# One of four sums of weights per pair by an accumulating load, with turned signs and a fourth raw buffer

## The chip, the cores and the metric

The kernel runs on 1 core of a Trainium2 chip. Its time is the device time of one execution in microseconds (us). TensorE (PE) does the matrix products, VectorE (DVE) and ScalarE (ACT) the work on elements, GpSimd (POOL) small things and some loads, and SyncE (SP) issues most of the loads from HBM.

## The reference

Two layers, each an FFN, a token mixer and a second FFN, with a layer norm behind each; 256 tokens of 1024 numbers in float32.

```python
D_MODEL = 1024; SEQ = 256; DEPTH = 2; D_FF = 2816

def swiglu(x, wg, wu, wd):
    return (jax.nn.silu(x @ wg) * (x @ wu)) @ wd

for l in range(DEPTH):
    x = layer_norm(ALPHA * x + 0.5 * swiglu(x, ffn_wg[l, 0], ffn_wu[l, 0], ffn_wd[l, 0]), ln_g[l, 0], ln_b[l, 0])
    m = token_mix(x, w_in[l], w_out[l], ...)
    x = layer_norm(ALPHA * x + m, ln_g[l, 1], ln_b[l, 1])
    x = layer_norm(ALPHA * x + 0.5 * swiglu(x, ffn_wg[l, 1], ffn_wu[l, 1], ffn_wd[l, 1]), ln_g[l, 2], ln_b[l, 2])
```

The token mixer (sparse attention, pooling, gated linear attention) is not touched by the change.

## The kernel before

**Products in three matmuls.** Each float32 operand is split in two, `h` and `l`: ACT copies it to the reduced type (`wh`, L217 or L229), DVE subtracts that from the original (`wl`, L218 or L230). A product is then three matmuls: high by high, high by low, low by high. All weights pass this way, 393 halves of 128x1024 (512 KB) in all: SP loads the half into a buffer `raw` (three of them, L222), ACT and DVE split it, and PE uses it for both halves of the tokens. The buffer is free for the next load when `wl` is done. `wh` and `wl` have rings of 8 buffers each.

**An FFN.** The 2816 columns of the hidden layer are 11 chunks of 256 gate and 256 up columns. `glu` (units `a`, `b` in the plan) makes one chunk from two weight units of two halves. `T0`, `T2`, ... transpose the gated result `hh` (or `cc`) of two chunks on PE and split it to `hi` and `lo` (L267, L268, called from `h_T`), and `d0`, `d1`, ... multiply it by the chunk's rows of the down weights and add to `accs`. `PLAN` (L41) is the order of these units on PE. It ends with `d7 T8`; then `end` runs d10, d8, d9 for the first 128 tokens, d10, d8, d9 for the others, and the layer norm (L342) follows each.

**Seven products for eight.** Three pairs of chunks per FFN (`S4`, `S6`, `S8`, so 12 pairs in all) are made by block products, "1 5 6 7 3 4 2" in this order, each of 12 matmuls. The inputs are cut in blocks of tokens and of inner index (`make_sums`, L310, forms the sums of x), the weights in b11, b12, b21, b22 of two halves each. `seven` (L135) forms the sums of weights: "5" takes b12 - b11, "6" takes b22 - (b12 - b11), "7" takes b22 - b12, "4" takes b21 less the sum of "6"; "1", "3" and "2" take b11, b22 and b21 as they are. Each sum is two DVE subtractions of 128x1024 (`less`, L145 to L147), in place in the tiles `fa` (b11) or `fb` (b12); `fc` is b22. b21 is loaded into two of the three `raw` buffers and stays there until "2" has been split. `plan` (L418) runs the products and adds up what PE leaves in PSUM (L462, L465, L468), and `gated` (L475) applies silu (ACT, L478) and the multiplication (DVE, L479).

**What sets the order.** Inside an FFN's plan PE's instructions are pinned to program order, and weight units are requested three ahead of their use, elsewhere one ahead. The order on the other engines is made by a scheduler when the kernel is built; on each engine it is then fixed, and an instruction that waits holds up all that stand behind it.

Of the kernel before, what the change touches and what calls it, by code (L numbers as in the profile page):

```python
# [10 lines left out]
def _warn_once_fixed(msg, *args, **kwargs):  # L11
# [7 lines left out]
F32 = mybir.dt.float32  # L19
# [3 lines left out]
AF = mybir.ActivationFunctionType  # L23
ALU = mybir.AluOpType
# [14 lines left out]


PLAN = ("a2 T0 b2 S4 1 a3 5 b3 6 T2 d0 7 d1 3 4 2 S6 d2 1 5 T4 d3 6 a10 7 b10 3 4 2 "  # L41
        "S8 1 d4 5 T6 6 d5 T10 7 d6 3 4 2 d7 T8").split()

LAST = (10, 8, 9)
WARM = ((7, 512), (4, 128))
# [12 lines left out]
def build(ctx, tc, d):  # L58
    nc = tc.nc
    PE, ACT, DVE, POOL = nc.tensor, nc.scalar, nc.vector, nc.gpsimd  # L60

    cst = ctx.enter_context(tc.tile_pool(name="cst", bufs=1))
    wp = ctx.enter_context(tc.tile_pool(name="wp", bufs=1))
# [54 lines left out]
    for t in range(2):  # L118
        vbd.append(cst.tile([128, 2, 2, 64], F32, name=f"vbd{t}"))
        a = cst.tile([128, 4, 128], F32, name=f"at{t}")  # L120
# [11 lines left out]
    def gate_up(l, f, c, q):  # L132
        return [d["wgu"][l, f, c, 2 * q + h] for h in range(2)]

    def seven(l, f, c):  # L135


        b11, b12, b21, b22 = [], [], [], []

        def load(to, src, pool, name, tags, bufs):  # L140
            for a, tag in zip(src, tags):
                to.append(pool.tile([128, 1024], F32, name=name, tag=tag, bufs=bufs))
                last_dma[0] = nc.sync.dma_start(out=to[-1], in_=a)

        def less(a, b, to):  # L145
            for x, y, z in zip(a, b, to):
                DVE.tensor_sub(out=z, in0=x, in1=y)  # L147

        def parts(ts):
            return [split_tile(x, 1024) for x in ts]  # L150

        def f1():
            load(b11, gate_up(l, f, c, 0), mix, "fa", ("qs0", "qs1"), 1)
            return parts(b11)

        def f5():
            load(b12, gate_up(l, f, c + 1, 0), wp, "fb", ("fb0", "fb1"), 1)
            less(b12, b11, b11)
            return parts(b11)

        def f6():
            load(b22, gate_up(l, f, c + 1, 1), mix, "fc", ("pT", "pT"), 3)
            less(b22, b11, b11)
            return parts(b11)

        def f7():
            less(b22, b12, b12)
            return parts(b12)

        def f4():  # L170
            load(b21, gate_up(l, f, c, 1), wp, "raw", ("raw", "raw"), 3)
            less(b21, b11, b11)
            return parts(b11)

        return {"1": f1, "5": f5, "6": f6, "7": f7, "3": lambda: parts(b22), "4": f4, "2": lambda: parts(b21)}

    for l in range(L):
        def ffn_units(f):
# [33 lines left out]
    def split_tiles():  # L212
        return (wp.tile([128, 1024], F32R, name="wh", bufs=8), wp.tile([128, 1024], F32R, name="wl", bufs=8))
# [5 lines left out]
        return wh, wl  # L219

    def split_half(src, w, parts=1, between=None):
        raw = wp.tile([128, 1024], F32, name="raw", bufs=3)  # L222
        wh, wl = split_tiles()
        for i in range(parts):
            s = slice(i * w // parts, (i + 1) * w // parts)
            last_dma[0] = nc.sync.dma_start(out=raw[:, s], in_=src[:, s])
            if between:
                between[i]()
            ACT.activation(out=wh[:, s], in_=raw[:, s], func=AF.Copy)  # L229
            DVE.tensor_sub(out=wl[:, s], in0=raw[:, s], in1=wh[:, s].bitcast(F32))  # L230
        return wh, wl
# [63 lines left out]
    def make_xT(t, qs=(0, 1), sums=None):  # L295
        if 0 in qs:
            XT[t] = (act.tile([128, 8, 128], F32R, name=f"xh{t}"), act.tile([128, 8, 128], F32R, name=f"xl{t}"))
        xh, xl = XT[t]
        for q in qs:
            p = transposes(t, [X[t][:, (4 * q + i) * 128:(4 * q + i + 1) * 128] for i in range(4)], ("tr", "acc")[q])  # L300
            split(xh[:, 4 * q:4 * q + 4, :], xl[:, 4 * q:4 * q + 4, :], p.rearrange("p (a b) -> p a b", a=4))
            if sums is not None:
                if (t, q) != (1, 1):
                    f = sums[t, q] = mix.tile([128, 512], F32, name=f"a{t}{q}", tag=("c40", "c41", "at011")[2 * t + q], bufs=1)
                    ACT.activation(out=f, in_=p, func=AF.Copy)
                else:
                    f = sums["s"] = mix.tile([128, 512], F32, name="s1", tag="vblk", bufs=1)
                    DVE.tensor_add(out=f, in0=p, in1=sums[1, 0])

    def make_sums(sums):  # L310

        s1, a11, a12, a21 = sums["s"], sums[0, 0], sums[0, 1], sums[1, 0]
        big = cst.tile([128, 2, 2, 4, 128], F32R, name="sb", tag="s_w1")

        def parts(f, i):
            tl = cst.tile([128, 2, 4, 128], F32R, name=f"sa{i}", tag=("ksh", "ksl")[i]) if i < 2 else big[:, i - 2]
            split(tl[:, 0], tl[:, 1], f.rearrange("p (a b) -> p a b", a=4))
            return tl[:, 0], tl[:, 1]
        first = parts(s1, 0)
        DVE.tensor_sub(out=s1, in0=s1, in1=a11)  # L320
        DVE.tensor_sub(out=a21, in0=a11, in1=a21)
        DVE.tensor_sub(out=a12, in0=a12, in1=s1)
        yield first
        yield parts(s1, 1)
        yield parts(a21, 2)
        yield parts(a12, 3)
# [39 lines left out]
    class Ffn:  # L366
# [51 lines left out]
        def plan(self):  # L418
            a = [[tuple(p[:, 4 * q:4 * q + 4] for p in XT[t]) for q in range(2)] for t in range(2)]
            left = {"1": a[0][0], "2": a[0][1], "4": a[1][1]}  # L420
            sums = make_sums(self.sums)

            def f32():
                self.cc += 1
                return mix.tile([128, 512], F32, name="cc", tag=("vblk", "cc", "c40", "at011", "c41")[self.cc % 5], bufs=1)

            def copy(b):

                r = f32()
                ACT.activation(out=r, in_=b, func=AF.Copy)  # L430
                return r
            for x in PLAN:
                if x[0] == "S":
                    c = int(x[1:])

                    (w1, b1), (w5, b5) = self.bank(), self.bank()
                    if not m0 and c == 8:
                        with tc.issue_after(last_dma[0].ins):
                            late_constants()
                            m0.append(Mix(0))  # L440
                            ln_params(0, 0)
                elif x[0] in "abTd":
                    for t in range(2):
                        if x[0] == "T":
                            self.h_T(t, int(x[1:]) // 2)
                        elif x[0] == "d":
                            self.down(t, int(x[1:]))
                        else:
                            self.glu(t, int(x[1:]), "ab".index(x[0]))
                    continue  # L450
                else:
                    if x in "5673" and x not in left:
                        left[x] = next(sums)
                    self.product(b1 if x in "1674" else b5, left[x], x in "152")
                with tc.high_priority():
                    if x == "1":
                        c11 = copy(b1)
                    elif x == "6":
                        u = copy(b1)
                    elif x == "7":  # L460
                        c22 = copy(b1)
                        DVE.tensor_add(out=c22, in0=b5, in1=c22)  # L462
                        self.gated(1, c + 1, c22)
                    elif x == "3":
                        DVE.tensor_add(out=u, in0=b5, in1=u)  # L465
                        self.gated(0, c + 1, u)
                    elif x == "2":
                        DVE.tensor_add(out=c11, in0=b5, in1=c11)  # L468
                        self.gated(0, c, c11)
                        self.free.append(w5)  # L470
                    elif x == "4":
                        self.gated(1, c, b1, f32())
                        self.free.append(w1)

        def gated(self, t, c, x, to=None):  # L475
            if to is None:
                to = x
            ACT.activation(out=to[:, 0:256], in_=x[:, 0:256], func=AF.Silu)  # L478
            DVE.scalar_tensor_tensor(out=to[:, 0:256], in0=to[:, 0:256], scalar=0.5, in1=x[:, 256:512], op0=ALU.mult,  # L479
                                     op1=ALU.mult)  # L480
            self.hh.setdefault((t, c // 2), [None, None])[c % 2] = to

        def h_T(self, t, g):
# [521 lines left out]
    sums = {}  # L1005
    for l in range(L):
# [3 lines left out]
        out = [wout(m, t) for t in range(2)]  # L1010
        for op in ORDER.split():
            t = int(op[1]) if len(op) > 1 else 0
# [16 lines left out]
        sums = nxt  # L1029
# [85 lines left out]
```

## Time and profile before

| | |
|---|---|
| time, median of 3 runs | 982.41 us (982.23 to 983.89) |
| the profiled execution | 982.67 us, of which the trace's span is 980.9 |
| PE, DVE, ACT, POOL busy | 959.1, 843.2, 583.1, 34.8 us |
| moved by DMA | 178.80 MB, mean 182 GB/s |
| granted clock of PE, mean | 0.997 |

The profile is that of one execution. Times in it count from the start of the span. The first FFN ends at about 186 us, its mixer at 320, the second FFN at 487, the third at 669, the second mixer at 803.

### The profile page before, as it was taken

How to read it: one execution, taken by the hardware profiler on the slowest of the kernel's cores; microseconds unless marked ns; L12 is line 12 of the kernel's file. 1: busy time of each engine (PE TensorE's matmuls, PEld its weight loads, DVE VectorE, ACT ScalarE, POOL GpSimd, SP SyncE). 2: the span in 40 equal slices, each digit the busy share in tenths (PEclk: the TensorE clock that was granted, in tenths of full speed). 3: DMA queues.
4: the chain of work that ended last, by engine and by line, in shares of the span. 5: the costliest groups of instructions: out<-in, count | busy, mean ns of one | idle time of the engine just before them, and what ended most of it. 6: DMA issues, size and time to landing. Idle time of an engine off the chain costs nothing. (4 is left out here: it accounts for less than half of the span.)

```text
span 980.9 us, 12843 instructions
## 1 busy us (share of the span) xinstructions
PE 959.1 (98%) x4611; PEld 780.5 (80%) x4611; DVE 843.2 (86%) x1247; ACT 583.1 (59%) x884; POOL 34.8 (4%) x50
## 2 busy tenths in 40 slices
PE   8999999999999999999999999999999999999996
PEld 5887888777778888888788888877787788888885
DVE  6798997887868988998899799978888699889986
ACT  6565664575764656565556666654667456556651
POOL 0000000020001000000000000001000010000000
PEclk9999999999999999999999999999999999999998
DMA  8765666564454645647673736466534364646251
GB/s 290 270 213 173 213 203 224 179 200 138 149 169 134 219 145 198 208 135 268 204 227 119 256 129 216 148 218 196 177 114 141 129 216 150 209 155 236 90 184 49
DMA packets 51872, 178.80 MB, mean 182 GB/s; under 512 B 6624, under 2 KB 7648, under 8 KB 51552
## 3 DMA queue, kind: packets, MB, share of 16 engines
q1 hardware_dynamic: 49968, 171.23, 52.8%
q0 software_dynamic: 1840, 6.75, 2.3%
q8 instruction: 36, 0.59, 0.2%
q14 instruction: 28, 0.23, 0.1%
HBM read 176.91 MB, written 1.05 MB: 181 GB/s over the span
## 5 line engine op out<-in xcount | busy, mean ns | idle before, releaser
L230 DVE TENSOR_TENSOR wl<-raw,wh 128x1024 fp32r<-128x1024 f32 (+2 forms) x225 | 267.7, 1202 | 60.5 <-ACT wh L229 59.8
L229 ACT ACTIVATE wh<-raw 128x1024 fp32r<-128x1024 f32 (+2 forms) x225 | 231.9, 1039 | 142.4 <-DMA raw<-in_wd 35.9
L217 ACT ACTIVATE wh<-fa 128x1024 fp32r<-128x1024 f32 x96 | 101.3, 1060 | 93.4 <-DVE fa L147 61.2
L262 PE MATMUL acc<-wh,hi 128*128 128x512 f32 x352 | 138.6, 394 | 0.0
L263 PE MATMUL acc<-wl,hi 128*128 128x512 f32 x352 | 137.2, 390 | 0.8 <-DVE wl L230 0.8
L264 PE MATMUL acc<-wh,lo 128*128 128x512 f32 x352 | 137.3, 390 | 0.0
L218 DVE TENSOR_TENSOR wl<-fa,wh 128x1024 fp32r<-128x1024 f32 x96 | 116.0, 1218 | 9.8 <-ACT wh L217 8.9
L263 PE MATMUL g<-wl,xh 128*128 128x512 f32 (+1 forms) x224 | 85.6, 382 | 1.6 <-DVE wl L230 1.6
L264 PE MATMUL g<-wh,xl 128*128 128x512 f32 (+1 forms) x224 | 86.3, 385 | 0.0
L262 PE MATMUL g<-wh,xh 128*128 128x512 f32 (+1 forms) x224 | 85.1, 381 | 0.0
L263 PEld LDWEIGHTS acc<-wl,hi 128*128 128x128 f32 x352 | 66.2, 188 | 14.5 <-DVE wl L230 1.1
L264 PEld LDWEIGHTS acc<-wh,lo 128*128 128x128 f32 x352 | 66.1, 188 | 13.9
L262 PEld LDWEIGHTS acc<-wh,hi 128*128 128x128 f32 x352 | 66.1, 188 | 13.8 <-ACT wh L229 0.4
L263 PE MATMUL acc<-wl,xh 128*128 128x512 f32 x128 | 51.5, 403 | 1.7 <-DVE wl L230 1.7
L262 PE MATMUL acc<-wh,xh 128*128 128x512 f32 x128 | 51.3, 402 | 1.1 <-ACT wh L229 1.1
L264 PE MATMUL acc<-wh,xl 128*128 128x512 f32 x128 | 50.5, 394 | 0.0
L262 PE MATMUL tr<-wh,xh 128*128 128x512 f32 x128 | 50.2, 392 | 0.0
L263 PEld LDWEIGHTS g<-wl,xh 128*128 128x128 f32 x224 | 42.1, 188 | 10.1 <-DVE wl L230 2.9
L264 PE MATMUL tr<-wh,xl 128*128 128x512 f32 x128 | 49.9, 390 | 0.0
L263 PE MATMUL tr<-wl,xh 128*128 128x512 f32 x128 | 49.8, 389 | 0.0
L262 PEld LDWEIGHTS g<-wh,xh 128*128 128x128 f32 x224 | 42.1, 188 | 8.2 <-issue 0.8
L264 PEld LDWEIGHTS g<-wh,xl 128*128 128x128 f32 x224 | 42.1, 188 | 6.9
(287 smaller groups left out, 1936.0 us busy)
## 6 DMA issues: line engine op xcount, KB each, us to landing
raw<-in_wgu SPq DMA_DIRECT2D x103, 512.0 KB, 4.1
raw<-in_wd SPq DMA_DIRECT2D x88, 512.0 KB, 4.5
raw<-in_win SPq DMA_DIRECT2D x32, 512.0 KB, 4.0
fa<-in_wgu SPq DMA_DIRECT2D x24, 512.0 KB, 4.1
fb<-in_wgu SPq DMA_DIRECT2D x24, 512.0 KB, 4.6
fc<-in_wgu SPq DMA_DIRECT2D x24, 512.0 KB, 4.8
raw<-in_wout SPq DMA_DIRECT2D x16, 512.0 KB, 3.8
lnp_ln_g<-in_ln_g POOLq DMA_DIRECT2D x5, 512.0 KB, 4.5
```

The costliest lines, as they stand in the source:

```text
L217: ACT.activation(out=wh[:, :w], in_=raw[:, :w], func=AF.Copy)
L218: DVE.tensor_sub(out=wl[:, :w], in0=raw[:, :w], in1=wh[:, :w].bitcast(F32))
L229: ACT.activation(out=wh[:, s], in_=raw[:, s], func=AF.Copy)
L230: DVE.tensor_sub(out=wl[:, s], in0=raw[:, s], in1=wh[:, s].bitcast(F32))
L262: pe(PE.matmul(ps, xh, wh, start=start, stop=False))
L263: pe(PE.matmul(ps, xh, wl, start=False, stop=False))
L264: pe(PE.matmul(ps, xl, wh, start=False, stop=stop))
```

## The change

- The sums change sign so that each is an addition: "5" takes b11 + b12 (into `fa`), "6" adds b22, "4" adds b21. "7" takes b12 + b22, and this sum is no longer made by DVE: when "5" has been formed, GpSimd issues two loads that add b22, read from HBM once more, to the tile that holds b12 (`fb`). Its 8 subtractions per pair become 6 additions, and the pair has two more loads of 512 KB.
- The sums of x in `make_sums` and `make_xT` get the signs that go with it, and `gated` gets a sign for the products "7" and "3".
- `raw` has four buffers, not three (b21 still takes two). The memory for GpSimd's DMA descriptors is halved.
- In `PLAN`, d4 of S8 moves from behind "1" to behind T6.

```diff
-        "S8 1 d4 5 T6 6 d5 T10 7 d6 3 4 2 d7 T8").split()
+        "S8 1 5 T6 d4 6 d5 T10 7 d6 3 4 2 d7 T8").split()
...
-        def less(a, b, to):
-            for x, y, z in zip(a, b, to):
-                DVE.tensor_sub(out=z, in0=x, in1=y)
+        def add(a, b):
+            for x, y in zip(a, b):
+                DVE.tensor_add(out=x, in0=x, in1=y)
...
             load(b12, gate_up(l, f, c + 1, 0), wp, "fb", ("fb0", "fb1"), 1)
-            less(b12, b11, b11)
+            add(b11, b12)
+
+            for x, a in zip(b12, gate_up(l, f, c + 1, 1)):
+                nc.gpsimd.dma_start(out=x, in_=a, accum_op=ALU.add)
             return parts(b11)
...
             load(b22, gate_up(l, f, c + 1, 1), mix, "fc", ("pT", "pT"), 3)
-            less(b22, b11, b11)
+            add(b11, b22)
             return parts(b11)
 
-        def f7():
-            less(b22, b12, b12)
-            return parts(b12)
-
         def f4():
-            load(b21, gate_up(l, f, c, 1), wp, "raw", ("raw", "raw"), 3)
-            less(b21, b11, b11)
+            load(b21, gate_up(l, f, c, 1), wp, "raw", ("raw", "raw"), 4)
+            add(b11, b21)
             return parts(b11)
 
-        return {"1": f1, "5": f5, "6": f6, "7": f7, "3": lambda: parts(b22), "4": f4, "2": lambda: parts(b21)}
+        return {"1": f1, "5": f5, "6": f6, "7": lambda: parts(b12), "3": lambda: parts(b22), "4": f4,
+                "2": lambda: parts(b21)}
...
-        raw = wp.tile([128, 1024], F32, name="raw", bufs=3)
+        raw = wp.tile([128, 1024], F32, name="raw", bufs=4)
...
-                    DVE.tensor_add(out=f, in0=p, in1=sums[1, 0])
+                    DVE.tensor_sub(out=f, in0=p, in1=sums[1, 0])
...
-        DVE.tensor_sub(out=s1, in0=s1, in1=a11)
+        DVE.scalar_tensor_tensor(out=s1, in0=s1, scalar=-1.0, in1=a11, op0=ALU.mult, op1=ALU.subtract)
         DVE.tensor_sub(out=a21, in0=a11, in1=a21)
-        DVE.tensor_sub(out=a12, in0=a12, in1=s1)
+        DVE.scalar_tensor_tensor(out=a12, in0=a12, scalar=-1.0, in1=s1, op0=ALU.mult, op1=ALU.subtract)
...
-                        self.gated(1, c + 1, c22)
+                        self.gated(1, c + 1, c22, sign=-1.0)
...
-            ACT.activation(out=to[:, 0:256], in_=x[:, 0:256], func=AF.Silu)
-            DVE.scalar_tensor_tensor(out=to[:, 0:256], in0=to[:, 0:256], scalar=0.5, in1=x[:, 256:512], op0=ALU.mult,
-                                     op1=ALU.mult)
+            ACT.activation(out=to[:, 0:256], in_=x[:, 0:256], func=AF.Silu, scale=sign)
+            DVE.scalar_tensor_tensor(out=to[:, 0:256], in0=to[:, 0:256], scalar=0.5 * sign, in1=x[:, 256:512],
+                                     op0=ALU.mult, op1=ALU.mult)
...
-    nc = bacc.Bacc("TRN2", target_bir_lowering=False, num_devices=1, dynamic_dma_scratch_size=8192)
+    nc = bacc.Bacc("TRN2", target_bir_lowering=False, num_devices=1, dynamic_dma_scratch_size=4096)
```

Where the instructions stand. (Lines of the changed kernel are one or two higher from L156 on.)

DVE in the first pair (S4) of the first FFN, before: `fb<-fc,fb` is the sum for "7", L218 and L230 are splits.

```order
L147 TENSOR_TENSOR fa<-fb,fa 128x1024 x2
L147 TENSOR_TENSOR fb<-fc,fb 128x1024
L401 SCALAR_TENSOR_TENSOR hh_447<-sg,tr_374 128x256
L218 TENSOR_TENSOR wl<-fa,wh 128x1024 x2
L230 TENSOR_TENSOR wl<-raw,wh 128x1024 x2
L147 TENSOR_TENSOR fa<-fc,fa 128x1024 x2
L147 TENSOR_TENSOR fb<-fc,fb 128x1024
L218 TENSOR_TENSOR wl<-fa,wh 128x1024 x2
L230 TENSOR_TENSOR wl<-raw,wh 128x1024 x2
L401 SCALAR_TENSOR_TENSOR hh_431<-sg,tr_479 128x256
L218 TENSOR_TENSOR wl<-fb,wh 128x1024 x2
```

The same place after:

```order
L147 TENSOR_TENSOR fa<-fa,fc 128x1024
L230 TENSOR_TENSOR wl<-raw,wh 128x1024
L402 SCALAR_TENSOR_TENSOR hh_449<-sg,tr_374 128x256
L230 TENSOR_TENSOR wl<-raw,wh 128x1024
L147 TENSOR_TENSOR fa<-fa,fc 128x1024
L218 TENSOR_TENSOR wl<-fa,wh 128x1024 x2
L230 TENSOR_TENSOR wl<-raw,wh 128x1024 x2
L218 TENSOR_TENSOR wl<-fb,wh 128x1024 x2
L147 TENSOR_TENSOR fa<-fa,raw 128x1024
```

The two sums for "7" are gone; the split of `fb` follows directly on the splits of the next units.

DVE at the end of the second FFN, before: `lo<-tr` is T8 for both halves of the tokens, L349 the start of the layer norm.

```order
L479 SCALAR_TENSOR_TENSOR cc<-cc 128x256
L230 TENSOR_TENSOR wl<-raw,wh 128x1024 x2
L268 TENSOR_TENSOR lo<-tr_4357,hi 128x512
L268 TENSOR_TENSOR lo<-tr_4366,hi 128x512
L230 TENSOR_TENSOR wl<-raw,wh 128x1024 x3
L349 SCALAR_TENSOR_TENSOR x_98<-x_98,acc_3457 128x512
```

The same place after:

```order
L230 TENSOR_TENSOR wl<-raw,wh 128x1024
L469 TENSOR_TENSOR cc<-g_4002,cc 128x512
L230 TENSOR_TENSOR wl<-raw,wh 128x1024 x2
L481 SCALAR_TENSOR_TENSOR cc<-cc 128x256
L230 TENSOR_TENSOR wl<-raw,wh 128x1024 x2
L268 TENSOR_TENSOR lo<-tr_4357,hi 128x512
L268 TENSOR_TENSOR lo<-tr_4366,hi 128x512
L350 SCALAR_TENSOR_TENSOR x_98<-x_98,acc_3457 128x512
```

The three splits between `lo` and the layer norm stand ahead of `lo` now: 196 splits of the program stood ahead of this `lo` before, 199 after. ACT's `hi` moves in the same way. In the first FFN it is 83 and 87, in the third 280 and 283, in the last 392 and 393.

GpSimd's queue in the first FFN, after; before, L124 was followed by the layer norm's power (L355) directly.

```order
L121 MEMSET at_86 128x512
L124 MEMSET grep 128x128
L161 DMA fb<-in_wgu 128x1024 x6
L356 ISA
L356 TENSOR_TENSOR ve_1648<-ve_1648,mhalf 128x1
```

The six accumulating loads of an FFN stand in a row and ahead of all that GpSimd does at the FFN's end.

## Rows read from the trace of the kernel before

**Rows 1.** Page, part 1: busy us, share of the span, instructions.

```profile
PE 959.1 (98%) x4611; PEld 780.5 (80%) x4611; DVE 843.2 (86%) x1247; ACT 583.1 (59%) x884; POOL 34.8 (4%) x50
```

**Rows 2.** Busy us by stretch; last: granted clock, DMA share, GB/s.

```profile
0.00:186.00 186.00, 180.63 (x806) 145.09 (x806) 157.56 (x175) 111.76 (x144) 1.67 (x11) 1.00 0.67 224
186.00:320.00 134.00, 130.79 (x732) 104.77 (x731) 110.03 (x278) 80.50 (x175) 15.33 (x19) 1.00 0.50 159
```

**Rows 3.** Timeline of PE: start us, us, line; product "1" of S8, then d4.

```profile
431.31 0.39 PE L415 MATMUL g<-wh,xh 128*128 128x512 f32 x1
...
434.03 0.39 PE L262 MATMUL acc<-wh,hi 128*128 128x512 f32 x1
```

**Rows 4.** Waits of PE: engine, line, releaser; us in total, times, longest.

```profile
PE acc L263 <- DVE wl L230: 2.5, 4, 1.0
PE tr L290 <- DVE x L360: 2.4, 2, 1.5
PE g L263 <- DVE wl L230: 1.6, 2, 0.8
...
PE tr L490 <- DVE cc L479: 1.2, 1, 1.2
PE acc L262 <- ACT wh L229: 1.1, 2, 0.7
...
PE tr L290 <- ACT c L584: 0.9, 1, 0.9
PE g L415 <- DVE cc L465: 0.8, 1, 0.8
```

**Rows 5.** Waits of PE in the first 20 us alone.

```profile
PE acc L263 <- DVE wl L230: 1.0, 1, 1.0
...
PE acc L262 <- ACT wh L229: 0.4, 1, 0.4
```

**Rows 6.** Waits of SP's queue; page, part 6: loads, count, KB, us to landing.

```profile
SPq L226 <- DVE wl L230: 451.0, 150, 11.5
...
raw<-in_wd SPq DMA_DIRECT2D x88, 512.0 KB, 4.5
```

**Rows 7.** Line L147 of DVE: count, ns min/median/max, first and last start.

```profile
L147 DVE TENSOR_TENSOR fb<-fc,fb x24: 1212/1216/1221, 46.8 to 924.6; 128x1024 f32<-128x1024 f32 x24
```

**Rows 8.** Timeline, S8 of the second FFN: sums and splits on DVE, "7" on PE.

```profile
430.32 1.22 DVE L147 TENSOR_TENSOR fa<-fb,fa 128x1024 f32<-128x1024 f32 x1
...
433.59 1.22 DVE L218 TENSOR_TENSOR wl<-fa,wh 128x1024 fp32r<-128x1024 f32 x1
...
451.77 0.48 PE L415 MATMUL g<-wh,sb 128*128 128x512 f32 x1
```

**Rows 9.** Line L337, loads that GpSimd issues: ns to issue, us to landing.

```profile
L337 POOL DMA_DIRECT2D lnp_ln_b<-in_ln_b x5: 527/530/546, 201.6 to 802.7; - x5
...
DMA to landing us min/median/max: 4.1/5.2/6.6
```

**Rows 10.** Timeline, end of the second FFN: d7, d10 on PE, split, layer norm.

```profile
460.81 1.22 DVE L230 TENSOR_TENSOR wl<-raw,wh 128x1024 fp32r<-128x1024 f32 x1
...
474.57 0.48 PE L262 MATMUL acc<-wh,hi 128*128 128x512 f32 x1
...
481.13 1.06 ACT L229 ACTIVATE wh<-raw 128x1024 fp32r<-128x1024 f32 x1 [0.81 <-DMA raw<-in_wgu]
...
482.23 1.23 DVE L230 TENSOR_TENSOR wl<-raw,wh 128x1024 fp32r<-128x1024 f32 x1 [0.64 <-ACT wh L229]
483.37 0.68 DVE L349 SCALAR_TENSOR_TENSOR x<-x,acc 128x512 f32<-128x512 f32 x1
```

**Rows 11.** Timeline, end of the first FFN: d7's split, `s_w`, d10 on PE.

```profile
159.98 1.22 DVE L230 TENSOR_TENSOR wl<-raw,wh 128x1024 fp32r<-128x1024 f32 x1
...
161.74 0.33 SPq L535 DMA_DIRECT2D s_w<-in_w  x1
...
173.22 0.48 PE L262 MATMUL acc<-wh,hi 128*128 128x512 f32 x1
```

More of the change, by code (lines that the diff above doesn't have):

```diff
@@ L462, in plan @@
                         DVE.tensor_add(out=c22, in0=b5, in1=c22)
-                        self.gated(1, c + 1, c22)
+                        self.gated(1, c + 1, c22, sign=-1.0)
                     elif x == "3":
                         DVE.tensor_add(out=u, in0=b5, in1=u)
-                        self.gated(0, c + 1, u)
+                        self.gated(0, c + 1, u, sign=-1.0)
                     elif x == "2":
@@ L473, in plan, with gated @@
                         self.free.append(w1)
-        def gated(self, t, c, x, to=None):
+        def gated(self, t, c, x, to=None, sign=1.0):
             if to is None:
                 to = x
-            ACT.activation(out=to[:, 0:256], in_=x[:, 0:256], func=AF.Silu)
-            DVE.scalar_tensor_tensor(out=to[:, 0:256], in0=to[:, 0:256], scalar=0.5, in1=x[:, 256:512], op0=ALU.mult,
-                                     op1=ALU.mult)
+            ACT.activation(out=to[:, 0:256], in_=x[:, 0:256], func=AF.Silu, scale=sign)
+            DVE.scalar_tensor_tensor(out=to[:, 0:256], in0=to[:, 0:256], scalar=0.5 * sign, in1=x[:, 256:512],
+                                     op0=ALU.mult, op1=ALU.mult)
             self.hh.setdefault((t, c // 2), [None, None])[c % 2] = to
```

## The prediction

> **What bounds the kernel now.** I read the totals first. TensorE (PE) is busy for 959.1 us of a span of 980.9, 98% [rows 1], VectorE (DVE) for 86% and ScalarE (ACT) for 59%. So the question is whether PE is short of work anywhere, not how busy DVE is. The stretches say where: PE is busy 180.63 us of the first 186 (an FFN, the start with its first loads included), and 130.79 of the 134 of the mixer, with a granted clock of 1.00 in both, which is 2.4 GHz [rows 2]. Inside the FFNs the matmuls of 512 columns follow each other without a gap, across the seam of two units too: twelve of product "1" from 431.31, and the first of unit d4 at 434.03, 2.72 us later, or 0.227 for one [rows 3]. There a shorter DVE queue buys nothing, because PE is not waiting for it.
>
> What is left is the list of PE's waits [rows 4]. Its seven rows that name a split (`wh`, `wl`), or something queued behind splits on ACT or DVE, sum to 10.5 us. 1.0 us of the row of L263 and 0.4 of the row of L262 belong to the start of the program [rows 5], which the change does not touch. The root of most of the rest is the raw buffer: SyncE's queue (SP) stood 451 us before raw loads until a `wl` had been subtracted and the buffer was free, and a load then takes 4.5 us to land [rows 6]. A chain of load 4.5, `wh` 1.06 and `wl` 1.23 [rows 10] is 6.8 us per buffer: three buffers give one split per 2.27 us, four one per 1.70.
>
> **The change part by part.** *The sum for "7" (L166 to L168).* 24 subtractions of 1.216 us go, 29.2 us of DVE [rows 7]. Bounds: 0 (PE is gapless where they ran) and all of 29.2. I take 0, since the seven waits together are a third of that.
>
> *The signs.* Four instructions per FFN change between tensor_tensor and scalar_tensor_tensor, and the silu gets a scale: no instruction is added. One of this size, 128x512, takes 0.68 us in the form that the change adds (at 483.37, [rows 10]), and two of them per FFN, all of it, would be 5.4 us of DVE if they were new; but each stands where a subtraction of the same size stood. Cost 0.
>
> *The accumulating loads.* Each pair gets two loads from GpSimd (POOL), 512 KB each, behind the two adds of product "5", and product "7" must have their result split. No row shows an accumulating load. The nearest are POOL's own plain loads of the same size: 0.53 us to issue and 4.1 to 6.6 us to land, 5.2 in the middle [rows 9]. I take 5.2 each, one after the other: 10.4 us, and 13.2 for the longest. The cover is tightest in S8: the second add starts at 430.32 and ends at 431.54, and PE comes to product "7" at 451.77 [rows 8]. That is 20.2 us, and the move of d4 does not change it, since the same matmuls lie ahead of "7". After the loads come one `wh` and one `wl`, 2.3 us, and the second half is needed 1.4 us later than the first. So 10.4 + 2.3 = 12.7 is hidden with 7.5 us and more to spare; the edge is at 19.3 us for both loads. Queued behind them are ACT's copy of `fb` and what follows on ACT, and SP's `fb` loads for the next pair, which wait for POOL's semaphores. Cost taken: 0.
>
> *The order in S8.* d4 goes behind "5" and T6, with its two loads on SP. PE now comes to product "5" directly after "1", at 434.03 instead of 5.4 us later [rows 3]. In the trace the splits of "5" are only just ready for that: the second one runs from 433.59 to 434.81 [rows 8], and its matmuls would start at 435.4, so 0.6 us is left. Taken at 0; a late one is a rival.
>
> *The fourth raw buffer.* Row by row of PE's waits [rows 4], I take back: 0.8 of 0.8 for L465 (its add stood behind a split that waited for a load), 1.0 of 1.2 for L479 and 0.7 of 0.9 for L584 (the silu and the copy stood behind a `wh` that waited for a load), 0.5 of the 0.7 at L262, 1.2 of the 1.5 at L263 outside the start, 0.2 of 1.6 for the `g` row of L263 (two splits in the mixers that stood behind DVE's other work, with their loads in place), and 2.4 of 2.4 for L360. This last row is the layer norm: at the end of the second FFN it starts at 483.37 behind a split that starts at 482.23 [rows 10], and in the new order no split stands there. Sum: 6.8 us.
>
> The new order asks a price for that. The three splits that stood between `lo` of T8 and the layer norm now stand ahead of that `lo` (four in the first FFN). PE needs this `lo` for d8, after the twelve matmuls of d10. Second FFN: d10 starts at 474.57 [rows 10], so the need is at 474.57 + 2.73 + 0.46 = 477.8. The fourth buffer of the ring is free when the second split of d7 ends, 460.81 + 2 x 1.22 = 463.25 [rows 10]. Two rounds of 6.8 us from there put the last of the splits ahead of `lo` at 476.85, and `lo`, 0.68 us, at 477.5. That is just in time; with loads that land in 5.2 it is 1.2 us late. I take 0.8. First FFN: the need is at 173.22 + 2.73 + 0.46 = 176.4, the buffer is free at 159.98 + 2.44 = 162.4, and two rounds, the last one with narrow tiles (6.0), give 175.2 and `lo` at 175.9. But the load of `s_w`, as large as two raw loads, is issued at 161.74 [rows 11], and 1 MB at the 224 GB/s of this stretch [rows 2] is 4.7 us: late by 0 to 4.2, and I take 1.7. Third FFN: 0.5 (0 to 2). Last FFN: one more split and nothing to load behind it, 0. Sum 3.0, between 0 and 8.2.
>
> **Sum.** 6.8 - 3.0 = 3.8 us. The profiled execution took 982.67, 0.26 above the median of 982.41; taken from the median, 978.6 us.
>
> **The rivals.** *A: the new waits eat the gain.* If the raw loads are bound by the traffic and not by the buffers, then the splits that stand ahead of `lo` arrive when they did, and the waits at d8 take 5 to 8 us. For it: the four loads in flight share 16 engines that are 67% taken in the first FFN [rows 2], and each pair now loads 1 MB more. Against: SP waits for buffers, 451 us [rows 6]. It gives 6.8 - 5 to 6.8 - 8.2, so 980.6 to 983.8.
>
> *B: the accumulating loads land late, slower.* The transfers may be held up by a DVE that is busy 157.56 of 186 us in the first FFN [rows 2], or by the add itself. The point is 19.3 us for both loads. At twice the longest landing, 13.2 each and in sequence, S8 is late by 26.4 + 2.3 - 20.2 - 1.4 = 7.1 us, four times: 28 us, about 1007. Against it: the loads of [rows 9] landed in at most 6.6 us beside a busy DVE. The Trainium skill, "SBUF — State Buffer", section "SBUF: two separate sides", states a rule that speaks against this change: a DMA issued by GpSimd waits for its descriptors while VectorE holds the port pair that the two share, and one that takes about 620 ns alone took about 3100. By that factor the 5.2 would be an estimated 26 us, and if both loads run together S8 would come to about the same 1007 us. The landings of [rows 9] show nothing of the kind, though the rule names VectorE copies, which the FFNs run few of.
>
> *C: product "5" of S8 comes too early, slower.* If one of its adds or splits slips by a split's period of 2.3 us, PE stands 2.3 - 0.6 = 1.7 us in each S8, 6.8 in all four. With A's waits beside them the balance is 6.8 - 8.2 - 6.8 = -8.2: about 990, and about 985 with the forecast's 3.0 of waits in their place. For it: 0.6 us of slack. Against: a shorter DVE queue moves these adds forward.
>
> *D: more is gained.* All splits come in time, no wait at d8: 982.4 - 6.8 = 975.6.
>
> **How the numbers follow.** The forecast, 976.6 to 980.4, gets 0.50; A 0.24; D 0.14; C 0.07; B 0.05. A measurement of this kernel tells about 0.2%, 2 us, from no change, so faster means below 980.4 and slower above 984.4. Faster is the forecast and D, 0.64; same is A, less a little that ends on either side, 0.24; slower is B and C, 0.12. The range runs from 975.0 (D's time) to 984.0 (A's upper end) and leaves out B, most of C and the far end of D.
>
> **What would show it.** In the trace of the changed kernel: DVE busy time down by about 29 us, PE's unchanged; the waits for L465, L479 (now L466, L481) and for the layer norm gone from PE's list; a new row, PE acc L263 or L264 waiting for `lo` L268 or `hi` L267, of about 3 us; accumulating loads that land in 4 to 7 us; ACT's `wh<-fb` with no wait for DMA that reaches PE. The prediction is wrong if PE's list names `wl<-fb`, or if PE's waits for d8 exceed 5 us, or if the waits that I take back are still there with their loads in place.

## The result and the profile after

The changed kernel takes 979.11 us (median of 8 runs, 977.41 to 980.87); the kernel before, run beside it, 983.25. The ratio is 0.9948 with an interval of 0.9926 to 0.997: faster by about half a per cent. The forecast was 978.6, with a range of 975.0 to 984.0. The profiled execution took 979.34 us, with a span of 977.6, which is 3.3 us less than before.

Part 1 of its page, the line that answers to [rows 1]:

```profile
PE 959.9 (98%) x4611; PEld 781.6 (80%) x4611; DVE 817.5 (84%) x1223; ACT 584.6 (60%) x884; POOL 55.7 (6%) x74
```

VectorE is busy 25.7 us less (the 24 subtractions alone took 29.2), TensorE 0.8 us more. So the VectorE time is not what the kernel got back. The waits of PE tell where the 3.3 us are; this list answers to [rows 4] (us in total, times, longest):

```profile
PE tr L492 <- DVE cc L481: 2.4, 1, 2.4
PE acc L290 <- DMA x<-in_x: 1.3, 1, 1.3
PE g L263 <- DVE wl L230: 1.3, 2, 0.6
PE acc L107 <- DVE zw L110: 1.2, 1, 1.2
PE acc L263 <- DVE wl L230: 1.0, 1, 1.0
PE tr L290 <- ACT c L641: 0.8, 2, 0.4
PE tr L667 <- PE acc L281: 0.7, 2, 0.4
PE acc L262 <- ACT wh L229: 0.7, 2, 0.4
```

The rows for L465, for the layer norm (L360) and for L584 are gone. What is left at L263 `acc` (1.0) and L262 (0.7) lies in the first 20 us. One row has grown, from 1.2 to 2.4 us: the transposes of T8 (L490, now L492) in the third FFN. There the trace shows one thing more. Granted clock (third from the right) in three stretches around it; the columns are those of [rows 2]:

```profile
640.00:649.80 9.80, 9.80 (x44) 7.84 (x42) 5.92 (x8) 4.20 (x7) 0.00 (x0) 1.00 0.90 330
649.80:652.20 2.40, 0.06 (x1) 0.00 (x0) 2.36 (x4) 2.22 (x4) 0.00 (x0) 1.00 0.26 35
...
653.00:656.50 3.50, 3.50 (x12) 2.82 (x10) 1.80 (x3) 1.03 (x2) 0.00 (x0) 0.52 0.94 323
```

PE stood for 2.4 us, went on at 652.28, and from 653.0 it ran for 3.5 us at 0.52 of its clock, the lower of its two levels (1.2 GHz). Its timeline has the price:

```profile
652.28 1.11 PE L492 MATMUL tr<-ident,cc 128*128 128x128 f32 x8 [2.42 <-DVE cc L481]
...
654.04 0.63 PE L264 MATMUL acc<-wh,lo 128*128 128x512 f32 x1
654.47 0.63 PE L262 MATMUL acc<-wh,hi 128*128 128x512 f32 x1
...
657.07 0.39 PE L263 MATMUL acc<-wl,hi 128*128 128x512 f32 x1
657.30 0.39 PE L264 MATMUL acc<-wh,lo 128*128 128x512 f32 x1
```

A matmul every 0.43 us and not every 0.23: eight of them, 1.6 us. Of the 8 runs four have a mean granted clock of 0.996, like the profiled one, and four of 0.998; their medians are 979.6 and 978.7, so this stretch is perhaps not in every run (only one was profiled). The balance of the two traces: PE's waits behind the start fall from 10.3 to 5.2 us, the start takes 0.4 more, the half clock 1.6. That is 5.1 - 0.4 - 1.6 = 3.1 of the 3.3 us.

The accumulating loads, line L161 (columns as in [rows 9]):

```profile
L161 POOL DMA_DIRECT2D fb<-in_wgu x24: 856/868/1019, 39.3 to 907.8; - x24
...
DMA to landing us min/median/max: 5.2/6.4/12.2
```

No row of PE names `wl<-fb`, and the view of L161 lists nobody that waited for these loads: they are hidden.

### The profile page after: what moved, and what is told of

It reads as the page before. It is cut to its first block, busy times and chain, and to the rows that moved or that the text cites. A ratio compares the mean times of both kernels' runs of the same rounds, so it can differ in the third digit from the quotient of the medians.

```text
span 977.6 us, 12931 instructions
## 1 busy us (share of the span) xinstructions
PE 959.9 (98%) x4611; PEld 781.6 (80%) x4611; DVE 817.5 (84%) x1223; ACT 584.6 (60%) x884; POOL 55.7 (6%) x74
## 4 chain that ended last, share of the span: by engine, by line
PE 93%; DVE 3%; DMA 1%; issue 1%; ACT 1%; SPq 0%; DVEq 0%; ACTq 0%
PE g L416 15%; PE acc L262 12%; PE acc L263 12%; PE acc L264 12%; PE tr L416 8%; PE g L262 4%; PE g L263 4%; PE g L264 4%; PE tr L264 3%; PE tr L262 3%; PE tr L263 3%; PE tr L290 3%; PE acc L281 2%; PE tr L492 1%; DVE wl L230 1%
## 5 line engine op out<-in xcount | busy, mean ns | idle before, releaser
L230 DVE TENSOR_TENSOR wl<-raw,wh 128x1024 fp32r<-128x1024 f32 (+2 forms) x225 | 267.3, 1202 | 52.8 <-ACT wh L229 50.9
L229 ACT ACTIVATE wh<-raw 128x1024 fp32r<-128x1024 f32 (+2 forms) x225 | 231.4, 1041 | 126.9 <-PE acc L264 68.5
L218 DVE TENSOR_TENSOR wl<-fa,wh 128x1024 fp32r<-128x1024 f32 x96 | 116.3, 1221 | 27.9 <-ACT wh L217 25.9
L262 PE MATMUL acc<-wh,hi 128*128 128x512 f32 x352 | 139.5, 396 | 0.0
L263 PE MATMUL acc<-wl,hi 128*128 128x512 f32 x352 | 137.7, 391 | 0.0
L263 PE MATMUL g<-wl,xh 128*128 128x512 f32 (+1 forms) x224 | 85.6, 382 | 1.3 <-DVE wl L230 1.3
L262 PE MATMUL g<-wh,xh 128*128 128x512 f32 (+1 forms) x224 | 85.2, 381 | 0.0
L263 PEld LDWEIGHTS acc<-wl,hi 128*128 128x128 f32 x352 | 66.6, 189 | 13.3
L262 PEld LDWEIGHTS acc<-wh,hi 128*128 128x128 f32 x352 | 66.5, 189 | 13.4
L263 PE MATMUL acc<-wl,xh 128*128 128x512 f32 x128 | 51.4, 401 | 1.0 <-DVE wl L230 1.0
L262 PE MATMUL acc<-wh,xh 128*128 128x512 f32 x128 | 51.0, 400 | 0.7 <-ACT wh L229 0.7
L262 PE MATMUL tr<-wh,xh 128*128 128x512 f32 x128 | 50.2, 392 | 0.0
L263 PE MATMUL tr<-wl,xh 128*128 128x512 f32 x128 | 49.8, 389 | 0.0
L263 PEld LDWEIGHTS g<-wl,xh 128*128 128x128 f32 x224 | 42.1, 188 | 9.5 <-DVE wl L230 2.1
L262 PEld LDWEIGHTS g<-wh,xh 128*128 128x128 f32 x224 | 42.2, 188 | 8.2 <-issue 0.8
```

What stands on the lines that cost most here:

```text
L218: DVE.tensor_sub(out=wl[:, :w], in0=raw[:, :w], in1=wh[:, :w].bitcast(F32))
L262: pe(PE.matmul(ps, xh, wh, start=start, stop=False))
L263: pe(PE.matmul(ps, xh, wl, start=False, stop=False))
```

## Experiments

The theory T: the fourth raw buffer brought the gain, and the DVE work that the accumulating loads replace was hidden. The rival D: the shorter DVE queue brought it. The first two runs are the two halves of the change.

**The fourth buffer alone, on the kernel before.**

```diff
-            load(b21, gate_up(l, f, c, 1), wp, "raw", ("raw", "raw"), 3)
+            load(b21, gate_up(l, f, c, 1), wp, "raw", ("raw", "raw"), 4)
...
-        raw = wp.tile([128, 1024], F32, name="raw", bufs=3)
+        raw = wp.tile([128, 1024], F32, name="raw", bufs=4)
...
-    nc = bacc.Bacc("TRN2", target_bir_lowering=False, num_devices=1, dynamic_dma_scratch_size=8192)
+    nc = bacc.Bacc("TRN2", target_bir_lowering=False, num_devices=1, dynamic_dma_scratch_size=4096)
```

> The kernel before with a fourth raw buffer alone (and the halved descriptor memory that makes room): the eight subtractions of a pair, the signs and the order of S8 stay. Theory T (the buffer brings the gain, the DVE sums were hidden): about the time of the changed kernel, 977.5 to 980, with the waits for L465, L360 (layer norm), L584 and the mixers' wh and wl at L262 and L263 gone from PE's list. Rival D (the shorter DVE queue brings half of the gain or more): 981 or more, with at least two of these waits still there.

Measured: 978.34 us (977.38 to 979.16), ratio 0.9945, 0.9923 to 0.9966. The whole gain is there without any of the rest. (The halved descriptor memory makes room for the buffer; the next run has it too, without the buffer.) PE's waits in it begin with a row that neither the kernel before nor the changed kernel has:

```profile
PE acc L264 <- DVE lo L268: 1.4, 2, 0.8
PE g L263 <- DVE wl L230: 1.3, 2, 0.6
```

That is the wait for `lo` of T8 that the prediction charged the new order with (counted between the starts of the matmuls, the gaps at the three places are 2.1 us). The profiled execution of the changed kernel doesn't have it, and so the DVE work is not worth nothing: it pays for most of this wait. Not for all of it in each run: with plain loads from GpSimd, below, there are 0.8 us of it in the first FFN.

**The changed kernel with three buffers.**

```diff
-            load(b21, gate_up(l, f, c, 1), wp, "raw", ("raw", "raw"), 4)
+            load(b21, gate_up(l, f, c, 1), wp, "raw", ("raw", "raw"), 3)
...
-        raw = wp.tile([128, 1024], F32, name="raw", bufs=4)
+        raw = wp.tile([128, 1024], F32, name="raw", bufs=3)
```

> The changed kernel with three raw buffers: accumulating loads, signs and order of S8 alone. Theory T: no gain, 981.5 to 983.5, with the waits on late raw loads back in PE's list. Rival D: 979 to 980.5, since 29 us less of DVE work lets the splits come earlier even with three buffers.

Measured: 982.15 us (979.91 to 984.65), ratio 0.9982, 0.9963 to 1.0: a third of the change's gain by the ratios, with an interval from none to 0.7 of it. Run beside it, the fourth buffer alone was 3.8 us faster, and its slowest run (979.16) was faster than the fastest of these (979.91). The layer norm's wait is gone here as well, but others are back or new, among them:

```profile
PE tr L290 <- ACT c L586: 1.8, 1, 1.8
...
PE tr L492 <- DVE cc L481: 1.3, 2, 0.7
...
PE acc L264 <- DVE lo L268: 0.8, 2, 0.6
```

T holds, D falls: the rest of the change may bring a part of the gain by itself, but adds nothing to that of the buffer that can be told.

**The place of d4.**

```diff
-        "S8 1 5 T6 d4 6 d5 T10 7 d6 3 4 2 d7 T8").split()
+        "S8 1 d4 5 T6 6 d5 T10 7 d6 3 4 2 d7 T8").split()
```

> The changed kernel with d4 of S8 back in its old place behind product 1. Theory: the place of d4 is worth nothing, within 1 us of the changed kernel (978 to 980), since the same matmuls lie ahead of product 7 either way. Rival: the old place takes cover from product 5 or the new one from product 7: a difference of 2 us or more and a new row for L416 in PE's waits.

Measured: 977.93 us (976.54 to 979.3), ratio 0.9942, 0.992 to 0.9964. No difference from the changed kernel that can be told, and no row for L416. The prediction took it at 0; the slack of 0.6 us at product "5" was enough.

**The wait that grew.** In the changed kernel the chain at T8 of the third FFN reads like this on GpSimd and ACT:

```profile
639.28 0.55 POOL L537 DMA_DIRECT2D s_w<-in_w  x1 [33.19 <-PE g L416]
...
643.22 1.06 ACT L229 ACTIVATE wh<-raw 128x1024 fp32r<-128x1024 f32 x1 [0.93 <-DMA raw<-in_wd]
648.23 1.06 ACT L229 ACTIVATE wh<-raw 128x1024 fp32r<-128x1024 f32 x1 [3.95 <-DMA raw<-in_wd]
649.49 1.06 ACT L229 ACTIVATE wh<-raw 128x1024 fp32r<-128x1024 f32 x1 [0.20 <-DMA raw<-in_wd]
650.45 0.40 ACT L480 ACTIVATE cc<-cc 128x256 f32<-128x256 f32 x1
```

The silu that T8 needs (650.45) stands behind two copies of raw halves, and the first of these waits 3.95 us for its load. The 1 MB load of `s_w`, which GpSimd issues at 639.28 as soon as its tile is free, is on the 16 engines at the same time; the stretch from 640 to 649.8, shown above, has them 90% busy. This was to be seen in the kernel before as well, where it cost 1.2 us:

```profile
653.42 1.06 ACT L229 ACTIVATE wh<-raw 128x1024 fp32r<-128x1024 f32 x1 [4.11 <-DMA raw<-in_wd]
654.39 0.40 ACT L478 ACTIVATE cc<-cc 128x256 f32<-128x256 f32 x1
```

With the fourth buffer alone a copy waits beside `s_w` too, but the silu stands ahead of it, and T8 has no row in PE's waits:

```profile
647.73 0.42 ACT L478 ACTIVATE cc<-cc 128x256 f32<-128x256 f32 x1 [0.42 <-DVE cc L468]
650.84 1.06 ACT L229 ACTIVATE wh<-raw 128x1024 fp32r<-128x1024 f32 x1 [2.69 <-DMA raw<-in_wd]
```

So it takes two things: a late load, and an order on ACT that puts the silu behind it. Up to this silu ACT has made 152 copies of L229 in the kernel before, 153 with either half of the change alone, and 155 with both. To test the first of the two, the load goes behind the raw loads on SP's queue:

```diff
             tl = cst.tile(shape, F32, name="s_" + nm)
-            q.dma_start(out=tl, in_=src)
+            if l and nm == "w1":
+                with tc.issue_after(last_dma[0].ins):
+                    nc.sync.dma_start(out=tl, in_=src)
+            else:
+                q.dma_start(out=tl, in_=src)
             s[nm] = tl
```

> The changed kernel, but in the second layer the 1 MB load of s_w is issued by SyncE behind the raw loads that the end of the FFN needs, not by GpSimd ahead of them. Theory S (the wait of 2.4 us at T8 of the third FFN, and the 3.5 us at half clock behind it, come from this load sharing the engines with a raw load): both vanish, 3 to 4.3 us less, about 975. Rival: the raw load is late without it too, or the wait moves to the product that uses s_w: 978 to 980.

Measured: 975.46 us (974.97 to 977.0), ratio 0.9919, 0.9897 to 0.994. The same copies in its trace:

```profile
644.41 1.06 ACT L229 ACTIVATE wh<-raw 128x1024 fp32r<-128x1024 f32 x1 [0.21 <-PE g L416]
646.40 1.06 ACT L229 ACTIVATE wh<-raw 128x1024 fp32r<-128x1024 f32 x1 [0.93 <-DMA raw<-in_wd]
647.37 0.40 ACT L480 ACTIVATE cc<-cc 128x256 f32<-128x256 f32 x1
```

The silu starts 3.1 us earlier, T8 has no row in PE's waits, and no stretch at half clock follows. By the medians this is 3.65 us from the changed kernel and by the ratios, each to the kernel before in the same series of runs, 2.9; the two traces lie 4.4 us apart, about the 2.4 + 1.6 that the changed kernel's showed. It has the lowest median of all kernels here.

**What the sums for "7" are worth then.** The same later load with the fourth buffer alone, on the kernel before (the two diffs above together):

> The kernel before with the fourth raw buffer and with the later load of s_w, without accumulating loads, signs and new order of S8. Theory T (the sums for 7 were hidden on DVE but for the waits for lo at three ends of FFNs, 2.1 us in the run with the fourth buffer alone): 976.5 to 977.5, that is 1 to 2 us above the changed kernel with the later load (975.46), and waits for lo L268 in PE's list. Rival (the sums are hidden wholly): 975 to 976, no wait for lo.

Measured: 976.31 us (975.94 to 978.5), ratio 0.9933, 0.9913 to 0.9953. That lies between my two expectations. It is 0.85 us above the run with the accumulating loads (1.4 by the ratios, from two series of runs), and the spreads overlap. One wait for `lo` is left, of 0.2 us. So taking the 24 subtractions from DVE, 29 us of its time, is worth about 1 us of the kernel's, and that it is more than nothing is not shown.

**The price of accumulating.** GpSimd's loads without the addition:

```diff
-                nc.gpsimd.dma_start(out=x, in_=a, accum_op=ALU.add)
+                nc.gpsimd.dma_start(out=x, in_=a)
```

> The changed kernel with plain loads from GpSimd in place of the accumulating ones; product 7 then takes b22 and not the sum. Theory: the addition costs the transfer little, and most of the difference between 6.4 us to landing here and 5.2 for GpSimd's other loads is the traffic beside it: 5.8 to 6.4 us to landing, issue near 0.87 us as well, same time (978 to 980). Rival: the addition costs it 1 us or more: 5.0 to 5.5 us, and issue near 0.55.

Measured: 979.24 us (978.12 to 982.96). The time is as I expected, the price of the addition is not: the issue is the rival's, and the landing is shorter than even the rival had it. The rows of L161 in this run:

```profile
L161 POOL DMA_DIRECT2D fb<-in_wgu x24: 527/527/689, 38.9 to 911.3; - x24
...
DMA to landing us min/median/max: 3.4/4.2/8.5
```

At the same places and beside the same traffic a plain load is issued in 0.53 us and lands in 4.2; the addition makes that 0.87 and 6.4. As both are hidden, the time is the same.

**The cover of the accumulating loads.** Each is issued two times, or four times, one behind the other:

```diff
-            for x, a in zip(b12, gate_up(l, f, c + 1, 1)):
-                nc.gpsimd.dma_start(out=x, in_=a, accum_op=ALU.add)
+            for _ in range(2):
+                for x, a in zip(b12, gate_up(l, f, c + 1, 1)):
+                    nc.gpsimd.dma_start(out=x, in_=a, accum_op=ALU.add)
```

> The changed kernel with each accumulating load issued twice, the second behind the first, so that product 7 takes b12 + 2 b22. The cover of the loads at double price: two of 6.4 us are 12.8, and ACT comes to its copy of fb 12 to 13 us after the issue. Theory: still hidden but for the traffic (12.6 MB more), 979 to 982. Rival B (the loads are near the path already): 985 or more, and PE waits for wl<-fb.

> The changed kernel with each accumulating load issued four times in sequence, so that product 7 takes b12 + 4 b22. 4 x 6.4 = 25.6 us is past the edge of 19.3 that the prediction put for S8. Theory: S8 late by 25.6 + 2.3 - 21.6 = 6.3 us, four times, and S6 by 2: about 30 us slower, 1005 to 1015, with ACT's wait for fb in the chain; more if the copy of fb, which holds up ACT's queue for some 13 us, stops other work. Rival (the edge is elsewhere, the loads overlap each other or are quicker): under 990.

Measured: 986.03 us twice (ratio 1.0028, 1.0011 to 1.0045) and 1143.86 four times. Both are worse than I expected, the second by far: 165 us above the changed kernel, not 30. With two the time is that of rival B, but not for its reason: no row of PE names `wl<-fb`; PE's listed waits are 3.3 us longer, of 6.0 us between the traces, and the rest is not traced. Waits of ACT, first of the run with two, then of the run with four (lines of these kernels are one higher than those of the changed kernel, so L218 is the copy of `fb`):

```profile
ACT wh L218 <- DMA fb<-in_wgu: 24.1, 15, 2.9
```

```profile
ACT wh L218 <- DMA fb<-in_wgu: 188.8, 24, 16.5
```

And what PE waits for with four:

```profile
PE tr L493 <- DVE hh L403: 47.8, 8, 13.1
PE g L417 <- ACT cc L432: 42.7, 4, 12.8
PE tr L417 <- ACT cc L432: 34.2, 4, 9.4
```

None of these rows names `fb`. PE does not wait for product "7"; it waits for copies out of PSUM (L432) and for gated chunks (`hh`), which stand on ACT and DVE behind the copy of `fb` that waits for its load. All of PE's waits in the run with four sum to 138 us, against 9.4 in the changed kernel; its mean granted clock is 0.929, against 0.996, so a part of the rest is the lower clock. The edge of the cover is therefore ACT's place in its own queue. In S8 of the second FFN of the changed kernel that is:

```profile
423.42 1.22 DVE L147 TENSOR_TENSOR fa<-fa,fb 128x1024 f32<-128x1024 f32 x1
...
425.17 0.86 POOL L161 DMA_DIRECT2D fb<-in_wgu  x1 [1.99 <-DVE fa L147]
...
437.06 2.01 ACT L217 ACTIVATE wh<-fb 128x1024 fp32r<-128x1024 f32 x2
```

From the end of the second add (424.64) to ACT's first copy of `fb` it is 12.4 us. From the issue of the second load it is 11.9, and 12.8 to that load's own copy, the second of the two. A load of 6.4 us leaves about 6 of it. In the two runs above a load takes 7.2 us (median): two in sequence exceed it a little, and four by some 16 us, close to the 15.7 us that ACT waits for `fb` per pair (188.8 in 12 pairs).

## Why the prediction was right, and where it was not

*The bound.* Right: PE was short of work in a few places only. The sum for "7" was taken at 0 of its 29.2 us, and the runs with and without it lie 0.8 us apart to one side (the fourth buffer alone is that much below the changed kernel) and 0.85 to the other (above it, with the later `s_w` in both).

*The signs* were taken at 0, and the two forms take the same time: 0.685 us in the trace after, and 0.684 for the subtraction that stood there before (two instructions per FFN change their form, not the four that the prediction counted):

```profile
L321 DVE SCALAR_TENSOR_TENSOR s<-s,a x4: 683/685/687, 18.1 to 806.4; 128x512 f32<-128x512 f32 x4
```

*The fourth buffer, row by row.* Predicted and measured: L465 0.8 and 0.8; L584 0.7 and 0.9; L262 0.5 and 0.7; L263 `acc` 1.2 and 1.5; L263 `g` 0.2 and 0.3; the layer norm 2.4 and 2.4. In these six rows the reading was right: they go with the fourth buffer alone, too. The seventh failed: for L479 I took back 1.0, and it lost 1.2, and 1.6 more at the half clock. With the fourth buffer alone this row is gone as well, as I had it. What I left out is that the other half of the change moves the silu two copies further back in ACT's queue, behind a copy whose load is late beside `s_w`; I had not looked at what that load shared the engines with. The run with the later `s_w` shows the second part; why the order on ACT shifts by these two copies was not tested by itself. Two waits of 0.4 us each (L641) are new, where the next late thing appeared; the run with the fourth buffer alone has them too (L639).

*The price of the new order.* Here the step failed in the other direction. I charged 3.0 us for the wait for `lo` at d8, and the trace of the changed kernel has none. The mechanism exists: 1.4 us of it in the run with the fourth buffer alone, 0.8 with three. What I got wrong is the place of the splits from which the rounds of 6.8 us are counted. I took it from the trace of before, where the first split of d7 starts 13 us ahead of T8. In the changed kernel the splits of b21, which stand ahead of those of d7 and free two of the four buffers, start earlier: the pair's DVE queue is shorter by two sums, and DVE works there almost without a pause. Second FFN, trace after (the split of b21, T8 and d10 on PE, then `lo` and the layer norm):

```profile
452.87 1.21 DVE L218 TENSOR_TENSOR wl<-raw,wh 128x1024 fp32r<-128x1024 f32 x1
...
469.81 1.04 PE L492 MATMUL tr<-ident,cc 128*128 128x128 f32 x8
470.60 0.48 PE L262 MATMUL acc<-wh,hi 128*128 128x512 f32 x1
...
472.42 1.28 DVE L268 TENSOR_TENSOR lo<-tr,hi 128x512 fp32r<-128x512 f32 x2
477.74 0.69 DVE L350 SCALAR_TENSOR_TENSOR x<-x,acc 128x512 f32<-128x512 f32 x1 [4.03 <-PE acc L264]
```

The second split of b21 starts 16.9 us ahead of T8. With the fourth buffer alone it is 14.1 as before:

```profile
455.61 2.36 DVE L218 TENSOR_TENSOR wl<-raw,wh 128x1024 fp32r<-128x1024 f32 x2
...
470.85 0.82 PE L490 MATMUL tr<-ident,cc 128*128 128x128 f32 x6
...
474.51 1.28 DVE L268 TENSOR_TENSOR lo<-tr,hi 128x512 fp32r<-128x512 f32 x2
```

(the second of the two starts at 456.7). Of these 2.8 us 1.1 arrive at `lo`, which starts 2.6 us behind T8 and not 3.7. That is enough: it starts at 472.42, and PE needs it at 470.60 + 2.73 + 0.46 = 473.8. The layer norm, at 477.74, waits for nothing but PE. I had priced an edit with the DVE queue of before, though another edit of the same change shortens it. In the first FFN the margin is small: of the runs made from the changed kernel with its four buffers three have a wait there, of 0.2 (d4 in its old place), 0.8 (plain loads) and 0.6 us (loads issued twice).

*The sum.* So the forecast of 3.8 us, against 4.1 by the medians and 3.3 by the two traces, owes something to two errors that nearly cancel: 3.0 us charged for `lo` and not paid, and 2.2 + 1.6 = 3.8 us at T8 that I did not charge. That the time came so near the forecast is luck; without the charge for `lo` the forecast would have been 975.6, with that for T8 added 982.4. (The upper ends of the four terms of the price, 1.2, 4.2, 2 and 0, add up to 7.4 us and not to 8.2, so A's upper end would be 983.0, and D's time of 975.6 stands as 975.0 in the range.)

*The accumulating loads.* Right that they are hidden, wrong in the two numbers. I took 5.2 us to landing and it is 6.4, as the addition costs 2.2 over the plain load at the same place. I put the edge at 19.3 us for both loads, by the time at which PE comes to "7", and it is at about 12 to 13, by the time at which ACT comes to `fb`. I had named ACT's queue as what stands behind the waiting copy and then did not use it. As priced, rival B at 26.4 us for both loads would have cost 28 us; the run with four in sequence, 25.6, cost 165.

The Trainium skill, "SBUF — State Buffer", section "SBUF: two separate sides", has a DMA issued by GpSimd wait for descriptors beside a VectorE copy, about 3100 ns for 620 alone. With VectorE 83% busy the plain loads of GpSimd landed in 4.2 us and SP's own loads of that size, `fb` from the same weights, in 5.0. The runs do not show the effect, and they do not test the rule: this kernel's VectorE work is mostly additions and subtractions of two operands and not copies.

*Open.* The kernel before spreads over 978.91 to 989.04 us in the three series of runs (8, 17 and 23), the changed kernel over 977.41 to 980.87 in 8. The differences of 1 us and less between kernels of different series are within that. What makes the slower of the former is not shown; the profile of before is of an execution of 982.67.

## What to carry to other kernels

When PE is gapless nearly everywhere, list its waits and ask of each what it stood behind and what that waited for: here one more buffer alone removed six of the seven rows outside the start, and 29 us of work taken from the busiest helper engine were worth about 1 us. A load that arrives late costs little where its consumer waits alone, and much where it holds an in-order queue: the slack of a new load ends where the first engine comes to it in its own queue, not where the product is needed. And price the edits of one change in the state, and in the order of the queues, that the others leave behind.

## What the runs showed of the hardware

The addition in a load of 512 KB costs about 2.2 us to landing (6.4 and 4.2) and 0.34 us of GpSimd's issue.

An idle PE can cost more than its wait. After 2.4 us of idleness in the changed kernel the granted clock was 0.52 for 3.5 us. After 2.1 us at the same place in the run with d4 in its old place it stayed at 1.00:

```profile
651.60:653.70 2.10, 0.20 (x1) 0.00 (x0) 1.97 (x4) 2.06 (x4) 0.00 (x0) 1.00 0.29 62
653.70:657.00 3.30, 3.08 (x18) 2.73 (x19) 2.73 (x5) 1.09 (x2) 0.00 (x0) 1.00 0.78 223
```

And with 3.9 us in the run with plain loads it was at 0.50 when PE went on:

```profile
655.20:658.70 3.50, 3.46 (x13) 3.10 (x14) 2.65 (x4) 1.19 (x2) 0.00 (x0) 0.50 0.85 264
```
